# Turning the softmax factors later, reordering the first products, and moving a few loads in a hybrid decoder block

## The chip, the core and the metric

The kernel runs on one core of a Trainium2 chip. A core has a matrix engine, TensorE (in the profile PE, with its weight loads apart as PEld), the vector engine VectorE (DVE), the scalar engine ScalarE (ACT), GpSimd (POOL) and SyncE (SP), whose queue issues most of the DMAs here; ScalarE's queue issues a few. The metric is the device time of one execution in microseconds.

## The reference, cut to what matters

The layer is a macaron block on 1024 tokens of width 1024, all in float32: half a SwiGLU feed-forward, a mixer, and half a second feed-forward, each behind an RMS norm, then a last norm.

```python
h = h + 0.5 * swiglu(rms_norm(h, ffn1_norm), w1, w3, w2)
u = rms_norm(h, mix_norm);  proj = u @ w_in          # q, k, v, p, gates
y_attn = dilated_mixture_attention(q, k, v) @ w_branch_attn
y_pool = multiscale_pool(pz, pool_w, pool_scale) @ w_branch_pool
merged = gates[0] * y_attn + gates[1] * y_pool
h = h + merged @ w_out
h = h + 0.5 * swiglu(rms_norm(h, ffn2_norm), ...)

# dilated_mixture_attention: three groups (window, dilation) of four heads
alpha = softmax(stack(log_denominators), axis=0)      # weights of the groups, per token and head
o = sum(alpha[..., None] * stack(group_outputs), axis=0)
```

The weights `alpha` of the groups are what the kernel calls factors.

## The kernel before, in words

**Products.** Every float32 operand is split into a high part and a low part (`hi`, `lo`), and a product is made of three: high by high, high by low, low by high (`three`, terms 0, 1 and 2, where the first factor is the weight). The large products use a scheme with seven half-size products; tiles are 128 x 512 into one PSUM bank. PSUM has eight banks in two rings of four, with the tags `mm` and `acc`.

**Order.** Inside `tc.manual_schedule()` each engine's instructions stand in the order in which the code emits them; outside of it a planner places them. Each engine, and SP's queue, works its own list in that order.

**The start.** `begin_up1` begins the first feed-forward while x and the first weights still arrive. `run_first(n, ks, terms)` (L1150) issues products of bank n (0 and 1, for two weight matrices) over the chunks ks of the contraction. The first call takes chunks 0 and 1, the second takes chunks 2 and 3 of bank 0 and then of bank 1. In x, `high` (L1057, ScalarE) makes xhi and `low` (L1066, VectorE) makes xlo. `split_low` (L1148, GpSimd) makes the weights' low parts.

**Attention.** 48 slots, one for a pair of heads hp (0, 1), a group g and a block i of 128 queries, are worked in 24 steps q of two slots each: `uses` are the six runs of eight slots. Step q issues in this order: `send()` (stores that are due), on even q the scores of q and q+1 (L1968), pieces of `combines`, a piece of the branch product (`fill`), the transposes of step q-1 (`trans_p`, L2015), more pieces of `fill`, the values of q-2 (L2048), the copy of q-3 out of PSUM (`gather`, L2071), the mask and the maxima (`masked`, L1986, VectorE), the split of the transposed scores of q-1 (ehi L2027 on ScalarE, elo L2030 on VectorE), splits of the next ring of queries and keys (L1590, L1591), `end_branches`, the exponents of both slots (L1995, ScalarE), and last `house` for each slot, which holds the loads and the steps of the factors.

**The factors of the first head pair.** `make_factors(0, gp)` (L1894) is a generator that `house` advances at the slots 32 to 36: the differences to the common maximum; their exponents; the factors (POOL, L1908 to L1912, with a reciprocal on VectorE); the transpose on TensorE (`f_turned`, L1917), its copy on ScalarE (L1919) and its store to DRAM (L1920, `f_by_head`); then four loads that spread the rows over the partitions (L1928, `f_of`). Slot 35 is the last of step q=17. At slot 36 `house` also issues the next values (`load_values`, L1611) and statistics (`get_stats`, L1889), behind the row loads.

**Their use.** `combine(0, half)` runs on GpSimd: per group a multiplication by f_of (L2081) and, from the second group on, an addition (L2085), then ScalarE's copy (L2090) and GpSimd's subtraction (L2091). The steps q = 20 to 23 advance the two halves; the last piece of half 1 stands behind the loop. The second head pair does the same on VectorE with factors that TensorE turns (`factor_rows`, L1946).

**The pooled branch.** `branches()` gives 48 pieces of four matmuls, three to a bank (L2110); behind each bank `end_branches` multiplies by the gate (`gb`, L2124, VectorE), and after each second one `send` stores the result (`by_pool`, L2134).

**Merges.** 16 merges each read a gate and a stored pool result (`load_merge`, L2161 and L2162). Loads 0 and 1 are issued behind the attention loop, load 2 in a closing loop over n = 0 to 7, loads 3 and 4 behind that loop, and from there each merge issues the load five ahead. The output projection (`wo`, L2368) takes its first operand from the first two merges; its split (o_hi L2355, o_lo L2356) is written behind merge 3.

**The second norm's gain** is loaded by `load_gain` (L206) on ScalarE's queue into a tile that held the attention's mask; outside the manual schedule.

Of the kernel before, what the change touches and what calls it, by code (L numbers as in the profile page):

```python
# [19 lines left out]
NT = S // P  # L20
# [117 lines left out]
def tile_block(  # L138
# [67 lines left out]
    def load_gain(src, name):  # L206
        t = keep.tile([P, D], F32, tag="gain", bufs=1, name=f"gain_{name}")
        nc.scalar.dma_start(t, src.to_broadcast([P, D]))
        return t
# [824 lines left out]
    def begin_up1():  # L1034
# [115 lines left out]
        def run_first(n, ks, terms):  # L1150
            if n not in banks:
                banks[n] = quads[n].bank["x"] = bank("mm", f"u_first{n}")
            w, (hi, lo) = first[n], X["b11"]
            for i in terms:
                for k in ks:
                    r = slice(k * P, (k + 1) * P)
                    a, b = three((w[:, 0, r], w[:, 1, r]), (hi[:, k, :], lo[:, k, :]))[i]
                    pe.matmul(banks[n], a, b, start=(k == 0 and i == 0), stop=(k == 3 and i == terms[-1]))

        FRONT, BACK = slice(0, 2 * P), slice(2 * P, HALF)  # L1160
        high("b11", 0, xt(0, 0), gain(0))
# [31 lines left out]
            high("b11", k, xt(0, k), gain(k))  # L1193
        for k in (2, 3):
            low("b11", k, xt(0, k), gain(k))
        run_first(0, (2, 3), (0, 2, 1))
        run_first(1, (2, 3), (0, 2, 1))
        operand(2, 1)
        operand(3, 1)
        high_b21(4)  # L1200
# [186 lines left out]
    class Mix:  # L1387
# [56 lines left out]
        def send(self):  # L1444
            for a in range(2):
                nc.sync.dma_start(gate_dram[self.g][:, a], self.y[a])
# [447 lines left out]
    def make_factors(hp, eng):  # L1894
# [19 lines left out]
        if hp == 0:  # L1914
            yield
            p = bank("mm", "f_turned")[:GROUPS * 2 * NT, :P]
            pe.transpose(p, by_head.rearrange("p g a i -> p (g a i)"), ident)  # L1917
            turned = att_small.tile([GROUPS * 2 * NT, P], F32, name="f_turned")
            ac.activation(turned, p, AF.Copy)  # L1919
            nc.sync.dma_start(f_dram.rearrange("g a i p -> (g a i) p"), turned)  # L1920
            yield
# [264 lines left out]
    def advance(gen, n=1):  # L2186
        for _ in range(n):
            next(gen, None)

    def house(s):  # L2190

        u, i = divmod(s, NT)
        if i == 1 and u > 0 and slots[s - 2][1] != 0:
            send_stats(*slots[s - 2][:2])
        if s - N // 2 in (8, 9, 10, 11, 12):
            advance(factors[0])
        if i == 4 and u + 1 < len(uses):
            load_values(uses[u + 1])
        if u > 0 and i == 4 and slots[s - 5][1] != 0:
            get_stats(*slots[s - 5][:2])  # L2200
        if N - 32 <= s < N - 13:
            advance(first)
        if s in (N - 6, N - 5, N - 4):
            load_ya(s - N + 6)

    first = first_w_o()
    with tc.manual_schedule():
# [6 lines left out]
                    for hp, (adds, lower) in enumerate((((gp, gp), gp), ((gp, ve), ve)))]  # L2214
        splits = {}
        for q in range(N // 2):
            send()
            if q % 2 == 0:
                scores(q)
                scores(q + 1)  # L2220
            for half in {20: (0, 0), 21: (0,), 22: (0, 1), 23: (1, 1)}.get(q, ()):
                advance(combines[0][half])
            if q == 0 or q % 2 == 1:
                next(fill, None)
            if q > 0:
                trans_p(q - 1)
                splits[q - 1] = split_p(q - 1)
                next(fill, None)
                if q % 4 == 1:
                    next(fill, None)  # L2230
            if q > 1:
                values(q - 2)
            if q > 2:
                gather(q - 3)
            masked(2 * q)
            masked(2 * q + 1)
            u, i = divmod(q, NT // 2)
            if 0 < u < len(uses) - 1 and i == 0:
                load_ring(uses[u + 1], ring_place(u + 1))
            if q > 0:  # L2240
                advance(splits[q - 1], 2)
            if i > 1 and 0 < u < len(uses) - 1:
                split_ring(uses[u + 1], i - 2)
                split_ring(uses[u + 1], i)
            end_branches()
            exponents(2 * q)
            exponents(2 * q + 1)
            if q in (2, 3):
                split_ring(uses[1], q - 2)
                split_ring(uses[1], q)  # L2250
            house(2 * q)
            house(2 * q + 1)
# [24 lines left out]
        for n in range(8):  # L2277
            advance(combines[1][n // 4])
            if n not in (3, 5, 7):
                next(fill, None)  # L2280
            end_branches()
            send()
            if n == 3:
                load_merge(2)
        for k in (3, 4):
            load_merge(k)
    assert next(fill, None) is None
    left_b.close()
    xstack.close()
# [3 lines left out]
    late["wc"] = ctx.enter_context(sbuf("wc2"))  # L2293
    late["xa"] = x2.enter_context(sbuf("x2a"))
    late["merged"] = m1.enter_context(sbuf("merged"))
    gain2 = load_gain(ffn2_norm, "ffn2")
    op = wo.enter_context(sbuf("ops", "right"))
    X2 = {}
    fs = ExitStack()
# [89 lines left out]
        return [Rows(X2, "b11", h[t][:, LOWS], t), Rows(X2, "b21", h[t][:, HIGHS], t)]  # L2389

    def scaled2(t):
        scaled(t, h[t] if t < 4 else rows_y[t], gain2)

    def lower(t, rs):
        for r in rs:
# [4 lines left out]
    with tc.manual_schedule():  # L2400
# [20 lines left out]
        for k in range(11, 16):  # L2421
            merge(k)
            if k in (12, 14):
                split_whole(2 + (k - 12) // 2, ve)
        sum_o(4)
        for t in range(4, NT):
            reload(t)
# [260 lines left out]
```

## Time and profile before

| what | value |
|---|---|
| median of 3 runs | 1876.27 us (1876.26 to 1876.63) |
| the profiled execution | 1877.42 us |
| its span, first to last instruction | 1875.2 us |
| TensorE clock granted | 0.999 |
| PE, PEld busy | 1863.7 us (99%), 1545.1 us (82%) |
| DVE, ACT, POOL busy | 1366.2 us (73%), 768.4 us (41%), 783.9 us (42%) |
| DMA | 339.70 MB, mean 181 GB/s |

A row of the timeline has the start and the duration in microseconds, the engine, the line of the kernel, the operation, the tile written and the tiles read, shapes and count, and in brackets how long the engine sat idle before and what released it. A row of the waits has the waiting instruction, the releaser, the total in microseconds, the number of waits and the longest. A row of the windows has a stretch of time and its length, the busy time and count of PE, PEld, DVE, ACT and POOL, then the granted clock, the DMA engines' share and GB/s. The ends of matmuls are modelled, so gaps are better seen in the weight loads.

### The profile page before, as it was taken

The page shows a single profiled execution, that of the slowest core. Times are in us where ns is not written, and L with a number is a line of the kernel's source. Part 1 is how long each engine was busy: PE and PEld are TensorE (multiplying, and loading weights), DVE is VectorE, ACT ScalarE, POOL GpSimd, SP SyncE. Part 2 cuts the span into 40 slices and gives each one's busy share as a digit, 9 for nine tenths or more (in the row PEclk, how much of TensorE's full clock was granted, in tenths as well). Part 3 has the DMA queues.
Part 4 walks back from the last instruction along what each step waited for, and adds up shares of the span by engine and source line. Part 5 has one row for each costly group of instructions (what it writes and reads, how often), then busy time and mean ns, then how long its engine had stood idle before and what let it go on. Part 6 is the DMA issues. An engine that isn't in the chain of part 4 may idle for free.

```text
span 1875.2 us, 24419 instructions
## 1 busy us (share of the span) xinstructions
PE 1863.7 (99%) x8667; PEld 1545.1 (82%) x8667; DVE 1366.2 (73%) x1966; ACT 768.4 (41%) x1393; POOL 783.9 (42%) x569
## 2 busy tenths in 40 slices
PE   9999999999999999999999999999999999999998
PEld 8888888888888888888888887888888888888886
DVE  7887866668886776658885886887765566577867
ACT  7422323233345643334445772463333333343344
POOL 5554644452222364445554467544333333312221
PEclk9999999999999999999999999999999999999999
DMA  8134324356565436765578888634332233354654
GB/s 327 45 124 149 121 95 152 117 206 209 192 231 198 157 114 208 258 211 185 213 251 324 314 254 298 267 129 180 120 139 85 90 107 122 126 203 157 223 197 146
DMA packets 148369, 339.70 MB, mean 181 GB/s; under 512 B 18024, under 2 KB 39576, under 8 KB 146712
## 3 DMA queue, kind: packets, MB, share of 16 engines
q1 hardware_dynamic: 144504, 327.30, 50.1%
q10 hardware_dynamic: 3744, 10.85, 1.6%
q8 instruction: 68, 1.11, 0.2%
q14 instruction: 53, 0.43, 0.1%
HBM read 237.48 MB, written 100.62 MB: 180 GB/s over the span
## 4 chain that ended last, share of the span: by engine, by line
PE 55%; DVE 2%; ACT 2%; DMA 1%; issue 1%; POOL 1%; SPq 0%; ACTq 0%; POOLq 0%; DVEq 0%
PE u_mixm L334 15%; PE d_f L904 8%; PE wo L2368 4%; PE yp L2110 2%; PE o L2048 1%; PE u_f20a L334 1%; PE u_f20b L334 1%; PE u_f21b L334 1%; PE u_f21a L334 1%; PE u_f210b L334 1%; PE u_f210a L334 1%; PE u_f29b L334 1%; PE u_f29a L334 1%; PE u_f28b L334 1%; PE u_f28a L334 1%; PE u_f27b L334 1%
## 5 line engine op out<-in xcount | busy, mean ns | idle before, releaser
L904 PE MATMUL d_f<-bhi_f,ahi_f 128*128 128x512 f32 x616 | 240.2, 390 | 0.0
L904 PE MATMUL d_f<-bhi_f,alo_f 128*128 128x512 f32 x616 | 239.8, 389 | 0.0
L904 PE MATMUL d_f<-blo_f,ahi_f 128*128 128x512 f32 x616 | 239.7, 389 | 0.0
L861 POOL TENSOR_TENSOR alo_f<-g_f,ahi_f 128x512 fp32r<-128x512 f32 x60 | 86.7, 1462 | 269.0 <-ACT ahi_f L857 269.0
L334 PE MATMUL u_mixm<-xhi_t_mix,wc_mixm 128*128 128x512 f32 x608 | 157.3, 391 | 0.1
L904 PEld LDWEIGHTS d_f<-bhi_f,alo_f 128*128 128x128 f32 x616 | 115.6, 188 | 24.3 <-DVE alo_f L861 0.2
L904 PEld LDWEIGHTS d_f<-bhi_f,ahi_f 128*128 128x128 f32 x616 | 115.6, 188 | 24.1 <-ACT h L424 0.5
L904 PEld LDWEIGHTS d_f<-blo_f,ahi_f 128*128 128x128 f32 x616 | 115.7, 188 | 24.0
L334 PEld LDWEIGHTS u_mixm<-xhi_t_mix,wc_mixm 128*128 128x128 f32 x608 | 113.5, 188 | 23.8 <-ACT wc_mixm L322 0.5
L334 PE MATMUL u_mixm<-xhi_b_mix,wc_mixm 128*128 128x512 f32 x456 | 120.3, 391 | 0.0
L325 POOL TENSOR_TENSOR wc_mixm<-s_mixm,wc_mixm 128x512 fp32r<-128x512 f32 x52 | 77.1, 1483 | 101.8 <-ACT wc_mixm L322 95.7
L334 PEld LDWEIGHTS u_mixm<-xhi_b_mix,wc_mixm 128*128 128x128 f32 x456 | 84.9, 188 | 17.2
L322 ACT ACTIVATE wc_mixm<-s_mixm 128x512 fp32r<-128x512 f32 x76 | 47.0, 628 | 111.4 <-DVE s_mixm L378 56.4
L857 ACT ACTIVATE ahi_f<-g_f 128x1024 fp32r<-128x1024 f32 x84 | 81.9, 975 | 6.8 <-DMA g_f<-gs_f 6.6
L334 PE MATMUL u_mixm<-xlo_t_mix,wc_mixm 128*128 128x512 f32 x304 | 81.3, 389 | 0.0
L325 POOL TENSOR_TENSOR wc_mixm<-raw,wc_mixm 128x512 fp32r<-128x512 f32 x41 | 62.3, 1522 | 37.9 <-ACT wc_mixm L322 24.6
L2368 PE MATMUL wo<-w_o,o_hi 128*128 128x512 f32 x224 | 69.4, 391 | 0.0
L646 POOL TENSOR_TENSOR y_f<-y_f,norm_ffn 128x512 f32<-128x512 f32 x35 | 54.4, 1560 | 35.5 <-DVE y_f L627 25.2
L857 ACT ACTIVATE bhi_f<-s_f2w 128x512 fp32r<-128x512 f32 x55 | 32.9, 627 | 86.0 <-DVE s_f2w L879 69.6
L857 ACT ACTIVATE bhi_f<-s_f1w 128x512 fp32r<-128x512 f32 x55 | 33.1, 629 | 83.5 <-DVE s_f1w L879 70.8
L334 PEld LDWEIGHTS u_mixm<-xlo_t_mix,wc_mixm 128*128 128x128 f32 x304 | 57.1, 188 | 12.0
L861 DVE TENSOR_TENSOR alo_f<-g_f,ahi_f 128x1024 fp32r<-128x1024 f32 (+1 forms) x48 | 58.6, 1222 | 7.7 <-ACT ahi_f L857 7.7
(1360 smaller groups left out, 4823.4 us busy)
## 6 DMA issues: line engine op xcount, KB each, us to landing
g_f<-gs_f SPq DMA_DIRECT2D x70, 512.0 KB
gs_f<-y_f SPq DMA_DIRECT2D x88, 256.0 KB
raw<-in_w2a_dram SPq DMA_DIRECT2D x35, 512.0 KB
raw<-in_w2b_dram SPq DMA_DIRECT2D x35, 512.0 KB
gs_f<-gb_f SPq DMA_DIRECT2D x46, 256.0 KB
raw<-in_w1b_dram SPq DMA_DIRECT2D x22, 512.0 KB
raw<-in_w3b_dram SPq DMA_DIRECT2D x22, 512.0 KB
raw<-in_w1a_dram SPq DMA_DIRECT2D x20, 512.0 KB
```

The costliest lines, as they stand in the source:

```text
L322: ac.activation(w[:, 0], src, AF.Copy)
L325: eng.tensor_tensor(w[:, 1], src, w[:, 0].bitcast(F32), op=OP.subtract)
L334: pe.matmul(p, a, b, start=(start and n == 0), stop=(n == 11), skip_group_check=not start)
L646: gp.tensor_tensor(c, c, self.sv.norm[:, cols], op=OP.mult)
L857: ac.activation(hi[:, c], src, AF.Copy)
L861: eng.tensor_tensor(lo[:, d], src[:, o], hi[:, d].bitcast(F32), op=OP.subtract)
L904: pe.matmul(self.banks[m][t], l, r, start=(first and q == 0), stop=(last and q == 2))
L2048: pe.matmul(p, l, r, start=(j == 0), stop=(j == end))
L2110: pe.matmul(p, a, b, start=(j == 0), stop=(j == 11))
L2368: pe.matmul(banks[m][t], l, r, start=(st == 0 and j == 0 and q == 0), stop=(st == 1 and j == 1 and q == 2))
```

## The change

- `run_first` for chunks 2 and 3: the terms 0 and 2 (those with xhi) of both banks first, then term 1 (with xlo) of both.
- The factors of the first head pair: the transpose moves from the end of step q=17 (slot 35) to the middle of step q=18, behind `trans_p`; a new `yield` parts it from the copy and the store, which move to slot 36, behind that step's exponents. The four row loads, and behind them the values and the statistics that slot 36 loaded, move to the head of q=19.
- The pieces of `combine` in q=22 and q=23 change places: two products of half 1 come first, then the last piece of half 0 with one of half 1.
- Merge loads 3 and 4 are issued in the closing loop, at n = 4 and n = 5.
- The gain of the second norm is loaded behind the last merge, inside the manual schedule.

```diff
@@ run_first
-                    pe.matmul(banks[n], a, b, start=(k == 0 and i == 0), stop=(k == 3 and i == terms[-1]))
+                    pe.matmul(banks[n], a, b, start=(k == 0 and i == 0), stop=(k == 3 and i == 1))
...
-        run_first(0, (2, 3), (0, 2, 1))
-        run_first(1, (2, 3), (0, 2, 1))
+        for terms in ((0, 2), (1,)):
+            for n in (0, 1):
+                run_first(n, (2, 3), terms)
@@ make_factors
             pe.transpose(p, by_head.rearrange("p g a i -> p (g a i)"), ident)
+            yield
             turned = att_small.tile([GROUPS * 2 * NT, P], F32, name="f_turned")
@@ house
-        if s - N // 2 in (8, 9, 10, 11, 12):
+        if s - N // 2 in (8, 9, 10, 12):
             advance(factors[0])
-        if i == 4 and u + 1 < len(uses):
+        if i == 4 and u + 1 < len(uses) and s != N // 2 + 12:
             load_values(uses[u + 1])
-        if u > 0 and i == 4 and slots[s - 5][1] != 0:
+        if u > 0 and i == 4 and slots[s - 5][1] != 0 and s != N // 2 + 12:
             get_stats(*slots[s - 5][:2])
@@ the attention loop
         for q in range(N // 2):
+            if 2 * q == N // 2 + 14:
+                advance(factors[0])
+                load_values(uses[(N // 2 + 12) // NT + 1])
+                get_stats(*slots[N // 2 + 7][:2])
             send()
...
-            for half in {20: (0, 0), 21: (0,), 22: (0, 1), 23: (1, 1)}.get(q, ()):
+            for half in {20: (0, 0), 21: (0,), 22: (1, 1), 23: (0, 1)}.get(q, ()):
                 advance(combines[0][half])
...
                 splits[q - 1] = split_p(q - 1)
+                if 2 * q == N // 2 + 12:
+                    advance(factors[0])
                 next(fill, None)
@@ the closing loop
             send()
-            if n == 3:
-                load_merge(2)
-        for k in (3, 4):
-            load_merge(k)
+            if n in (3, 4, 5):
+                load_merge(n - 1)
@@ the gain
-    gain2 = load_gain(ffn2_norm, "ffn2")
...
-        scaled(t, h[t] if t < 4 else rows_y[t], gain2)
+        scaled(t, h[t] if t < 4 else rows_y[t], late["gain"])
...
                 split_whole(2 + (k - 12) // 2, ve)
+        late["gain"] = load_gain(ffn2_norm, "ffn2")
         sum_o(4)
```

## The prediction

> **What bounds the kernel now.** I read the page first: the shares of the engines beside the span.
>
> ```profile
> span 1875.2 us, 24419 instructions
> ## 1 busy us (share of the span) xinstructions
> PE 1863.7 (99%) x8667; PEld 1545.1 (82%) x8667; DVE 1366.2 (73%) x1966; ACT 768.4 (41%) x1393; POOL 783.9 (42%) x569
> ```
>
> TensorE is busy for all but 11.5 us (1875.2 - 1863.7). An edit that takes no matmul away can win only gaps in that stream, so I went next to the view of waits, for the weight loads, where gaps show a little larger than in the modelled matmuls.
>
> ```profile
> PEld wo L2368 <- DVE o_lo L2356: 1.6, 2, 1.2
> PEld u_first L1158 <- DVE xlo_b_f L1066: 1.4, 1, 1.4
> PEld o L2048 <- DVE elo L2030: 1.3, 2, 0.8
> PEld idle L1041 <- DVE fours L1042: 1.1, 1, 1.1
> PEld f_turned L1917 <- POOL f L1912: 0.8, 1, 0.8
> ```
>
> Columns: total us, times, longest. Three of these lie where the diff works: u_first (the first products of the first feed-forward), f_turned (the turned softmax factors), and wo (the output projection, whose first operands come out of the merges). Together they are 1.4 + 0.8 + 1.6 = 3.8 us, and 0.2% of 1876.27 is 3.75 us, which is about what a measurement of this kernel can tell from no change. So even the whole of them would barely show.
>
> **Part 1, the first products.** The stall in the timeline of matmuls (start, duration), and GpSimd's last split of the weights:
>
> ```profile
> 11.75 0.50 PE L1158 MATMUL u_first<-xlo_b_f,wc_first 128*128 128x512 f32 x1 [0.98 <-DVE xlo_b_f L1066]
> 12.09 1.10 PE L1158 MATMUL u_first<-xhi_b_f,wc_first 128*128 128x512 f32 x4
> 13.03 0.62 PE L1158 MATMUL u_first<-xlo_b_f,wc_first 128*128 128x512 f32 x2
> 13.49 0.40 PE L334 MATMUL u_f11a<-xhi_b_f,wc_f11a 128*128 128x512 f32 x1
> ```
>
> ```profile
> 7.93 1.44 POOL L1148 TENSOR_TENSOR wc_first<-raw,wc_first 128x256 fp32r<-128x256 f32 x2
> ```
>
> Nothing is added or removed; 12 matmuls are reordered. Before, bank 0 runs its four products with xhi, then its two with xlo, and the second of these waits until 11.75; only then come the six of bank 1. After, the four xhi products of bank 1 stand ahead of all xlo products. Their weights were ready at 7.93 + 1.44 = 9.37, so they fill the gap. Four matmuls cost 13.03 - 12.09 = 0.94 us and the gap in matmuls is 0.98, so **-0.94**; the last xlo is still awaited at 11.75. Bounds: -0.98 if the gap closes wholly, and 0 if the lead is lost again, for which there is a place:
>
> ```profile
> 58.21 0.53 PEld L334 LDWEIGHTS u_f10a<-xhi_t_f,wc_f10a 128*128 128x128 f32 x3 [0.51 <-ACT wc_f10a L322]
> ```
>
> Here TensorE waits for ScalarE. If ScalarE's work there is paced by TensorE, it comes 0.94 earlier too; if not, the wait grows from 0.51 to 1.45. I take -0.94, since the waits view names no DMA as releaser of TensorE anywhere.
>
> **Part 2, the factors.** Before, the turn, its ScalarE copy and its store stand at the end of an odd step (q=17); TensorE waits for GpSimd there. After, the transpose stands behind the next step's own transposes, the copy behind that step's exponents, and the four row loads at the head of q=19. What moves: one matmul, one ACTIVATE and eight transfers on SP's queue (the store, four row loads, and behind them two value loads and one of statistics). The SP rows, then the ScalarE rows at which the new copy will stand, and the VectorE row that gives a score bank back:
>
> ```profile
> 1096.83 0.33 SPq L1920 DMA_DIRECT2D f_by_head<-f_turned  x1
> 1097.27 0.36 SPq L2134 DMA_DIRECT2D by_pool<-gb  x1
> 1098.31 2.61 SPq L1928 DMA_DIRECT2D f_of<-f_by_head  x4
> ```
>
> ```profile
> 1101.65 0.19 ACT L1995 ACTIVATION_READ_ACCUMULATOR e<-e,own_stats 128x1 f32 x1
> 1102.26 0.60 ACT L2027 ACTIVATE ehi<-tp 128x512 fp32r<-128x512 f32 x1 [0.42 <-PE tp L2015]
> ```
>
> ```profile
> 1097.98 0.08 DVE L1986 DVE_READ_ACCUMULATOR2_ANT own_stats<- 128x1 f32 x1
> ```
>
> The stall of 0.8 goes, so the step runs 0.8 earlier. The exponents end at 1101.84 - 0.8 = 1101.04. The copy is taken at 0.3 and hides in ScalarE's idle 0.42. The transpose now comes behind the four banks of scores and needs the first of them back, which VectorE has read at 1098.06 today; at most 0.8 (the whole win) is lost on that, and I take nothing, since TensorE's next transposes wait for the exponents anyway. The store goes out at about 1101.3, and the first row load follows as before by 1098.31 - 1096.83 = 1.48, at 1102.8: 4.5 us later than now. The by_pool store, queued behind the factors' store today, passes it.
>
> Who waits for the rows? GpSimd's eleven operations that combine the first head pair:
>
> ```profile
> 1096.00:1098.00 2.00, 1.80 (x26) 1.60 (x27) 1.51 (x9) 0.27 (x1) 0.15 (x1) 1.00 0.05 12
> 1098.00:1102.00 4.00, 3.89 (x23) 2.95 (x23) 2.96 (x9) 3.17 (x11) 2.14 (x2) 1.00 0.67 228
> 1102.00:1106.00 4.00, 4.00 (x40) 3.55 (x41) 3.49 (x16) 3.17 (x11) 2.93 (x4) 1.00 1.07 240
> ```
>
> ```profile
> 1103.46 2.53 POOL L1591 TENSOR_TENSOR xhi_b_mix<-xhi_b_mix,xlo_b_mix 128x512 fp32r<-128x512 f32 x2 [1.07 <-ACT xlo_b_mix L1590]
> 1105.94 2.56 POOL L2081 TENSOR_TENSOR o<-o,f_of 128x512 f32<-128x512 f32 x2
> ...
> 1113.24 1.27 POOL L2091 TENSOR_TENSOR att<-o,att 128x512 fp32r<-128x512 f32 x1 [0.74 <-ACT att L2090]
> ...
> 1119.73 1.29 POOL L2085 TENSOR_TENSOR o<-o,o 128x512 f32<-128x512 f32 x1
> ```
>
> The last columns of the windows are the DMA share and GB/s. Today GpSimd starts at 1105.94, straight behind its earlier work, and ends the chain at 1119.73 + 1.29 = 1121.02, 15.08 later with a wait of 0.74 inside. The first half needs two of the four row loads: by the code 64 x 3 x 512 x 4 bytes each, 0.79 MB for two. At the mean of 228 and 240 GB/s that is 3.4 us, and the store issued at 1097.27 moved hardly a byte before 1098.0, which I read as 0.7 of start-up. So the rows land at about 1102.8 + 0.7 + 3.4 = 1106.9. The reordered pieces (half 0 is finished behind the first products of half 1) take the 0.74 out, so the chain ends at 1106.9 + 15.08 - 0.74 = 1121.2, against 1121.02. Does the end of this chain matter?
>
> ```profile
> 1121.06 0.63 ACT L2090 ACTIVATE att<-o 128x512 fp32r<-128x512 f32 x1
> 1121.56 0.34 ACTq L208 DMA_DIRECT2D gain_ffn<-in_ffn_norm_dram  x1
> 1121.60 0.58 ACT L2027 ACTIVATE ehi<-tp 128x512 fp32r<-128x512 f32 x1
> ```
>
> ```profile
> 1124.69 2.00 ACT L1937 ACTIVATE f_of<-f 128x1024 f32<-128x1024 f32 x2 [1.89 <-DVE f L1912]
> ...
> 1125.93 0.35 PEld L1946 LDWEIGHTS fa<-ident,f_of 128*128 128x128 f32 x3
> ```
>
> It does: ScalarE copies its result (L2090, within 0.04 of GpSimd's end), then splits the last scores (ehi), behind which VectorE makes the second pair's factors, ScalarE spreads them, and TensorE turns them at 1125.93. The first of the two copies at 1124.69 ends about 1125.7, so 0.2 is free. A chain 0.2 later less 0.2 free leaves fa where it was, and the 0.8 won at q=18 is waited out here: **0.0**. Bounds: -0.8 if nothing in this chain binds; +3.3 by the first rival below. The activation that finishes half 0 (0.63, as L2090 at 1121.06) moves from q=22 to q=23 with its GpSimd subtraction; it stands ahead of the same kind of work, and its price is in the sum of the eleven operations.
>
> The row was 1.48 from a store to the reads of what it wrote. The Trainium skill ("DMA: Bandwidth & Descriptors", section "Anatomy of one DMA") gives a fixed cost of some 2.0 us for a DMA, most of it until the written data is confirmed; by that the rows would come 0.5 later and this part would cost 0.5 instead of nothing. I go by the row.
>
> The two value loads behind the rows (1.05 MB) are used here:
>
> ```profile
> 1115.24 0.28 PE L2048 MATMUL o<-ehi,v_in 128*128 128x256 f32 x1
> ```
>
> Rows and values are 2.6 MB, through by 1102.8 + 0.7 + 11.2 = 1114.7 at the same rate, against 1115.24 - 0.8 = 1114.4; the 0.3 comes out of the same 0.8.
>
> **Part 3, the merge loads.** Loads 3 and 4 are written into the loop over n, at n = 4 and 5, rather than behind it. Is there a store between? These rows tell:
>
> ```profile
> 1133.30 0.68 DVE L2083 TENSOR_TENSOR o<-o,fa 128x512 f32<-128x512 f32 x1
> 1133.89 0.68 DVE L2124 TENSOR_TENSOR gb<-yp,gb 128x512 f32<-128x512 f32 x1
> 1134.50 0.68 DVE L2083 TENSOR_TENSOR o<-o,fa 128x512 f32<-128x512 f32 x1
> ```
>
> ```profile
> 1134.60 0.32 SPq L2134 DMA_DIRECT2D by_pool<-gb  x1
> ```
>
> The last branch's product (gb) stands between the multiplications of n = 4 and n = 5, so its store is issued by the send of n = 4: 48 branch pieces, 42 taken in the main loop, two behind it, four at n = 0, 1, 2, 4. In the new code the load of n = 4 still comes behind that send. The queue of SP keeps its order, store then loads, and the 1.6 us at wo stay: **0.0**, at best -1.6.
>
> **Part 4, the gain.** Its load leaves ScalarE's queue at 1121.56 (0.34, overlapping two activations that run back to back there) and goes behind the last merges. It moves 128 x 1024 x 4 bytes, 0.52 MB, 2.2 us of DMA time at the 234 GB/s above, in either place. It is not used before the norm that follows the output projection, so only its company can suffer: **0.0**, at most 0.3 either way (about its 0.34 on ScalarE).
>
> **Sum.** -0.94 + 0.0 + 0.0 + 0.0 = -0.94 on the profiled execution: 1877.42 (span 1875.2 and 2.2 around it) becomes 1876.5. That execution lies 1.15 above the median 1876.27; the same step from the median gives **1875.3**.
>
> **Rivals.** *The rows come late, and the kernel gets slower.* If GpSimd's first multiplication needs all four row loads, or the stream runs at half its rate, they land at 1102.8 + 0.7 + 6.7 = 1110.2 and the chain ends at 1110.2 + 14.34 = 1124.5, which is 3.5 later than now, less 0.2 free = +3.3; with -0.94 that is +2.4, or 1878.7. It decides from a start of 1107.8 on, where the chain's delay passes 0.94 + 0.2. For it: SP's store comes 4.4 late into a DMA stream that is full (share 1.07). Against it: today GpSimd starts at 1105.94, when 0.91 + 0.96 = 1.87 MB had moved since 1098.0, less than the store and four row loads (2.1 MB), so it cannot have waited for all four. The Trainium skill's advice (same page, "Rules for kernel authors") to issue a DMA early and wait for it late speaks for this rival, too: the reads move towards their user.
>
> *The start's gain is lost at 58.21*, where ScalarE may not follow: total 0.0, 1876.3. *The 0.8 is kept*, when the end of the attention isn't bound by GpSimd's chain: -1.74, 1874.5. For it, nothing waits visibly at 1125.93; against it, the 0.04 between GpSimd and ScalarE. *The merge loads do pass the store*, against my count: -0.94 - 1.6 gives 1873.7.
>
> **Chances.** Forecast 0.55; late rows 0.15; start lost 0.12; 0.8 kept 0.13; merge loads 0.05. The range reaches from 1874.3, just under the case that keeps 0.8, to 1877.4, half way into the late rows; the forecast's own is 1874.9 to 1875.8. None of the cases crosses 0.2%: faster than 1872.5 needs two best cases at once (0.02), slower than 1880.0 late rows and late values together (0.04), so 0.94 for no change.
>
> **What would show it.** Right: u_first gone from the waits or under 0.3, u_f11a starting near 12.55; no wait at f_turned; the store of f_by_head near 1101 less the start's lead; GpSimd's first multiplication of L2081 near 1106; SP's order store, merge, merge unchanged and wo waiting as before. Wrong: a GpSimd wait of over 2 us for a DMA before L2081, a wait of TensorE at fa or at values of q=22 above 1 us, or merge loads ahead of the store.

## The result, and the profile after

The changed kernel takes 1879.28 us (median of 20 runs, 1878.00 to 1880.68) and the kernel before 1876.26 us on the same chip (20 runs, 1875.23 to 1877.89): a ratio of 1.0015, with a 95% interval from 1.0009 to 1.0021. It is 3.0 us slower where 0.94 less was forecast (under the 0.2% that the prediction took as the least that can be told, yet the interval leaves out 1), and it lies beyond the range's upper end, near the rival in which the rows come late (1878.7). The profiled execution after took 1878.00 (span 1875.8), the quickest of its kernel; the one before took 1877.42, near the slow end of its range. The two spans differ by 0.6 only, so the profiles were taken a second time below. Line numbers after are one higher from L1199 on, two higher from L1920 to L2216, and five or more higher behind that.

The waits of the profile after, in the stretch from 1090 to 1150 us (total, times, longest):

```profile
POOL o L2083 <- DMA f_of<-f_by_head: 4.5, 1, 4.5
ACT att L2092 <- POOL o L2087: 2.2, 1, 2.2
DVE top L1904 <- DMA stats<-st: 1.6, 1, 1.6
PEld fa L1948 <- ACT f_of L1939: 1.5, 1, 1.5
PEld o L2050 <- DMA v_in<-v: 1.4, 1, 1.4
PEld wo L2373 <- DVE o_lo L2361: 0.6, 1, 0.6
PEld f_turned L1918 <- issue: 0.3, 1, 0.3
```

The stall at f_turned has shrunk from 0.8 to 0.3. In its place stand three waits for transfers: GpSimd for the rows of factors, TensorE for the values of q=22, VectorE for the statistics of the last group (the second head pair's factors need them). GpSimd's wait and TensorE's two are the prediction's own signs of "wrong". The queues of SP and GpSimd in that trace, and its windows (last columns: granted clock, DMA share, GB/s):

```profile
1099.84 0.33 SPq L1922 DMA_DIRECT2D f_by_head<-f_turned  x1
1101.32 2.59 SPq L1930 DMA_DIRECT2D f_of<-f_by_head  x4
...
1117.76 0.38 SPq L1890 DMA_DIRECT2D stats<-st  x1
```

```profile
1108.34 2.55 POOL L2083 TENSOR_TENSOR o<-o,f_of 128x512 f32<-128x512 f32 x2 [4.54 <-DMA f_of<-f_by_head]
...
1121.29 1.29 POOL L2087 TENSOR_TENSOR o<-o,o 128x512 f32<-128x512 f32 x1
```

```profile
1096.00:1102.00 6.00, 5.87 (x41) 4.74 (x39) 5.17 (x20) 5.27 (x18) 3.27 (x3) 1.00 0.03 8
1102.00:1104.00 2.00, 2.00 (x28) 1.83 (x26) 1.96 (x9) 1.36 (x8) 1.80 (x2) 1.00 0.34 106
1104.00:1106.00 2.00, 2.00 (x13) 1.75 (x12) 1.77 (x5) 2.00 (x8) 0.00 (x0) 1.00 0.88 226
1106.00:1108.00 2.00, 2.00 (x13) 1.73 (x12) 1.96 (x7) 1.52 (x5) 0.00 (x0) 1.00 1.06 221
```

The transfer engines stand idle for six microseconds (share 0.03) because the store waits for ScalarE's copy, which now comes behind the exponents. Then the rows take 7.0 us from the first load's issue (1101.32) to GpSimd's start (1108.34). GpSimd's chain ends at 1122.58, and the profile shows what hangs on it, ScalarE first, then TensorE:

```profile
1122.62 0.63 ACT L2092 ACTIVATE att<-o 128x512 fp32r<-128x512 f32 x1 [2.21 <-POOL o L2087]
1123.15 1.07 ACT L2029 ACTIVATE ehi<-tp 128x512 fp32r<-128x512 f32 x2
1124.11 0.24 ACT L1907 ACTIVATE w<-w 128x48 f32<-128x48 f32 x1
```

```profile
1127.34 0.66 PE L1948 MATMUL fa<-ident,f_of 128*128 128x128 f32 x4 [1.26 <-ACT f_of L1939]
```

### The profile page after: what moved, and what is told of

The parts are those of the page before. It is cut to its first block, busy times and chain, and to the rows that moved or that the text cites. A ratio compares the mean times of both kernels' runs of the same rounds, so it can differ in the third digit from the quotient of the medians.

```text
span 1875.8 us, 24418 instructions
## 1 busy us (share of the span) xinstructions
PE 1863.3 (99%) x8667; PEld 1544.1 (82%) x8667; DVE 1364.0 (73%) x1966; ACT 768.3 (41%) x1393; POOL 784.2 (42%) x569
## 4 chain that ended last, share of the span: by engine, by line
PE 53%; DVE 2%; DMA 2%; ACT 2%; issue 1%; POOL 1%; SPq 0%; ACTq 0%; DVEq 0%; POOLq 0%
PE u_mixm L334 15%; PE d_f L904 8%; PE wo L2373 4%; PE u_f20a L334 1%; PE u_f21b L334 1%; PE u_f20b L334 1%; PE u_f21a L334 1%; PE u_f210b L334 1%; PE u_f210a L334 1%; PE u_f29b L334 1%; PE u_f29a L334 1%; PE u_f28b L334 1%; PE u_f28a L334 1%; PE u_f27b L334 1%; PE u_f27a L334 1%; PE u_f26b L334 1%
```

## The experiments

All times are medians; a ratio is to the kernel before, timed beside it on the same chip, with its 95% interval. Each profile is of one execution. There are four theories. **G** (first called R): the rows are late, GpSimd's chain behind them ends late, and that sets the end of the attention. **Q**: the transfers form one line from the first row to the last group's statistics, so those come late as well, and VectorE's wait sets the end. **V**: TensorE's wait for the values does; **C**: the loss is in the closing part.

### Each part alone

`e_start` is Part 1 alone, `e_factors` Part 2 alone, `e_late` Parts 3 and 4 alone, `e_no_factors` Parts 1, 3 and 4; their diffs are those pieces of the change.

> Part 1 alone, everything else as before. Theory R (the rows of factors land late and GpSimd's chain behind them sets the end of the attention) and theory V (the values of q=22 land late and TensorE's wait for them sets it) both say that the loss of the changed kernel is all in Part 2, and the start keeps what the trace after shows from u_f11a on: 1.2 us ahead of before, through the whole kernel, 1875.1 us. Theory C (the loss is in the closing part: the merge loads and the gain) says the same. If the lead is lost where before already waited for transfers (merge loads, 2.1 us on VectorE at the end of the attention), the time is that of before, 1876.3.

> Part 2 alone, without the 1.2 us that Part 1 gives. Theory R: the first row load is issued near 1102.5, two row loads land 6.9 us behind it, GpSimd starts near 1109.4 and ends its chain 14.2 us later near 1123.7, fa is 2.7 us behind before: 1878.1 where the closing part gives 0.9 back as in the trace after, up to 1880.5 where it gives nothing back and the median of after is carried over. Theory V: the stall of 1.0 at f_turned goes, a wait of 1.65 for the values comes: 1876.9. Theory C: nothing, 1876.3 or 1.0 less.

> Parts 3 and 4 alone. Theories R and V: no change, 1876.3 +- 0.5, with the order store, merge, merge on SP as before. Theory C: the loss of the changed kernel is here, 1878.5 or more, with a longer wait for a merge load or for the gain.

> Parts 1, 3 and 4 together, Part 2 left as before. Theories G and Q: the whole loss goes; the sum of what Part 1 alone (0.3 under before) and Parts 3 and 4 alone (0.7 under before) gave is 1.0 under before, 1875.2; 1876.0 if the 0.7 was chance. Any loss left against before would mean that the parts hinder each other.

| kernel | median | before | ratio |
|---|---|---|---|
| e_start | 1875.90 | 1876.22 | 0.9999 (0.9990 to 1.0008) |
| e_factors | 1880.27 | 1876.22 | 1.0022 (1.0014 to 1.0031) |
| e_late | 1875.55 | 1876.22 | 0.9997 (0.9988 to 1.0006) |
| e_no_factors | 1875.54 | 1876.74 | 0.9996 (0.9987 to 1.0005) |

Part 2 alone costs 4.05; the other parts give 0.3 and 0.7, which no interval tells from nothing. The sum, 4.05 - 0.3 - 0.7 = 3.05, is the loss of the changed kernel. C falls. The 1.2 us expected of Part 1 didn't come either, and the start of `e_factors`, which doesn't hold Part 1, says why: there u_f11a begins at 12.55, though it began at 13.49 before.

### The same two kernels profiled again

> The kernel before, profiled a second time, because its start in the runs of Part 2 alone and of Parts 3 and 4 alone has no gap of 0.98 us at u_first though Part 1 isn't in them. If that gap belongs to the one execution profiled first: u_f11a starts near 12.5 instead of 13.49, VectorE's wait for a merge load at the end of the attention is near 1.0 instead of 2.1, span near 1874. If it belongs to the kernel: 13.5 and 2.1 again, span 1875.

> The changed kernel, profiled a second time. Theory G (GpSimd's chain behind the late rows alone sets the end of the attention): GpSimd idle 4 to 5 us for the rows, fa 1.4 behind the first profile of before, as in the first profile of after. Theory Q (one transfer queue runs without a gap from the first row to the statistics of the last group, so each microsecond by which the first row starts later reaches those statistics, and VectorE's wait for them sets the end as often as GpSimd does): VectorE waits 1.6 to 3.3 us for the statistics at its factors, and fa comes between 1.4 and 2.7 behind.

One execution each: before 1876.73 (span 1874.5), after 1880.84 (span 1878.6). The opening in the timeline of matmuls, second profile of before:

```profile
10.82 0.50 PE L1158 MATMUL u_first<-xlo_b_f,wc_first 128*128 128x512 f32 x1
11.16 1.10 PE L1158 MATMUL u_first<-xhi_b_f,wc_first 128*128 128x512 f32 x4
12.11 0.62 PE L1158 MATMUL u_first<-xlo_b_f,wc_first 128*128 128x512 f32 x2
12.56 1.09 PE L334 MATMUL u_f11a<-xhi_b_f,wc_f11a 128*128 128x512 f32 x4
```

and the profile after:

```profile
11.39 1.08 PE L1158 MATMUL u_first<-xlo_b_f,wc_first 128*128 128x512 f32 x4
12.31 1.07 PE L334 MATMUL u_f11a<-xhi_b_f,wc_f11a 128*128 128x512 f32 x4
```

The gap of 0.98 isn't there the second time. It belonged to one execution. Over all profiles u_f11a starts at 12.25 on average with Part 1 (15 of them, 12.02 to 12.55) and at 12.50 without (four, the first left out): Part 1 is worth about 0.25 at this place; that it reaches the end isn't shown. VectorE's wait for a merge load at the end of the attention was 1.8 in the second profile of before, not near 1.0 as expected, and 0.6 to 2.6 over all of them: it, too, changes from run to run.

The same matmul's start, second profile of before taken as zero (negative is ahead):

| where | after | after, again |
|---|---|---|
| step 17, ahead of the factors | -0.23 | -0.07 |
| step 20, the stall at f_turned gone | -1.23 | -1.06 |
| behind the values of q=22 | +0.41 | +0.77 |
| fa | +2.29 | +3.39 |
| first output projection, behind the merges | +1.82 | +3.88 |

So the lead won at f_turned is 1.0, and about 3.5 and 4.5 are lost from there to fa. VectorE and GpSimd in the second profile of after show what the first hid:

```profile
1120.37 1.16 DVE L1903 TENSOR_TENSOR top<-stats 128x16 f32<-128x16 f32 x1
1123.55 0.18 DVE L1904 TENSOR_TENSOR top<-top,stats 128x16 f32<-128x16 f32 x1 [2.02 <-DMA stats<-st]
1123.76 1.19 DVE L1905 TENSOR_TENSOR w<-top,stats 128x48 f32<-128x48 f32 x1
```

```profile
1121.57 1.28 POOL L2087 TENSOR_TENSOR o<-o,o 128x512 f32<-128x512 f32 x1
1123.60 1.29 POOL L2093 TENSOR_TENSOR att<-o,att 128x512 fp32r<-128x512 f32 x1 [0.74 <-ACT att L2092]
```

```profile
1124.99 0.24 ACT L1907 ACTIVATE w<-w 128x48 f32<-128x48 f32 x1 [0.49 <-DVE w L1905]
```

The same steps of VectorE and ScalarE in the second profile of before, where neither waits (lines one lower):

```profile
1120.12 0.18 DVE L1903 TENSOR_TENSOR top<-top,stats 128x16 f32<-128x16 f32 x1
```

```profile
1121.58 0.24 ACT L1906 ACTIVATE w<-w 128x48 f32<-128x48 f32 x1
```

In the second profile of after GpSimd ends its chain at 1122.85, but the exponential of the second factors comes only at 1124.99, straight behind VectorE's L1905 (1123.76 + 1.19 = 1124.95). In the first profile it came at 1124.11, behind ScalarE's own split. Two chains end within a microsecond of each other, and either can be last.

### The copy moved, early or late

`v_early`: the changed kernel with the copy and store behind ehi, and rows, values and statistics in slot 36 again.

```diff
-        if i == 4 and u + 1 < len(uses) and s != N // 2 + 12:
+        if i == 4 and u + 1 < len(uses):
...
-        if u > 0 and i == 4 and slots[s - 5][1] != 0 and s != N // 2 + 12:
+        if u > 0 and i == 4 and slots[s - 5][1] != 0:
...
-            if 2 * q == N // 2 + 14:
-                advance(factors[0])
-                load_values(uses[(N // 2 + 12) // NT + 1])
-                get_stats(*slots[N // 2 + 7][:2])
...
                 advance(splits[q - 1], 2)
+            if 2 * q == N // 2 + 12:
+                advance(factors[0])
```

> The changed kernel with the copy and the store of the factors directly behind step 18's first ScalarE copy (behind ehi, ahead of the operand splits and the exponents), and rows, values and statistics back in slot 36. Theory R: copy near 1097.0 instead of 1099.55, first row load near 1098.8 instead of 1101.3, rows land near 1105.7, GpSimd ends near 1120.0, so fa comes 1.0 us ahead of before instead of 1.4 behind: 1875.3, or 1.0 below before's median of the same chip. Theory V: values land 2.5 us sooner too, TensorE keeps its lead of 2.2: 1874.1 if nothing else binds. Theory C: no change from after, 1879.3.

1878.42, ratio 1.0009 (1.0000 to 1.0018): about a quarter of the loss goes, not all of it. TensorE's wait for the values is gone, and fa came at 1127.01, hardly sooner than after (1127.34): V falls. SP waited longer for the factors' store (the first row load was issued 2.40 behind it instead of 1.48), so that load went out at 1099.83; and VectorE waited 3.3 us for the statistics.

`b_copy_late`: the kernel before, with only the copy moved behind the exponents of step 18, and rows, values and statistics to the head of step 19.

```diff
             pe.transpose(p, by_head.rearrange("p g a i -> p (g a i)"), ident)
+            yield
...
+            if 2 * q == N // 2 + 14:
+                advance(factors[0])
+                load_values(uses[(N // 2 + 12) // NT + 1])
+                get_stats(*slots[N // 2 + 7][:2])
```

> The kernel before with one step of Part 2 alone: the copy and the store of the factors come behind step 18's exponents, and rows, values and statistics at the head of step 19, while the transposition with its stall of 0.8, the order of the combines and everything else stay. Theories G and Q: this alone brings the whole loss, because TensorE's lead wasn't on the path: the first row load near 1102.5 and fa 2.5 to 3.5 behind before: 1879.5 (1879 to 1880.5). If the mere lateness of the transfers costs less than 1.5, the rest of Part 2 (the order of the combines, the transposition's new place) has a share of its own.

1881.59, ratio 1.0026 (1.0015 to 1.0037): the late copy alone brings the whole loss and 2 us more than the changed kernel. The size was missed: without the lead of the other edits the copy came at 1101.78, and a second wait appeared, ScalarE's for GpSimd's first half in step 22:

```profile
1117.24 0.63 ACT L2091 ACTIVATE att<-o 128x512 fp32r<-128x512 f32 x1 [5.35 <-POOL o L2086]
```

`v_old_order`: the changed kernel with the combines as before.

```diff
-            for half in {20: (0, 0), 21: (0,), 22: (1, 1), 23: (0, 1)}.get(q, ()):
+            for half in {20: (0, 0), 21: (0,), 22: (0, 1), 23: (1, 1)}.get(q, ()):
```

> The changed kernel with the combines in the order of before (first half's copy and subtraction in step 22, second half's last two multiplications in step 23). GpSimd stood idle 0.74 us for ScalarE's copy there in the trace of before, and doesn't in the trace after. Theory G: GpSimd ends 0.7 later, fa 2.1 behind the first profile of before instead of 1.4: 1880.0. Theory Q: where VectorE's wait for the statistics decides, nothing changes: between 1879.3 and 1880.0. If ScalarE waits in step 22 for GpSimd's first half and the exponents behind it come late, TensorE loses up to 2 us of its lead, which isn't on the path either.

1879.53, ratio 1.0015 (1.0006 to 1.0024): the time of the changed kernel. ScalarE waits 5.4 us for GpSimd in step 22, and GpSimd's chain is 15.0 long instead of 14.2; fa came at 1128.20, between the two profiles of after. The new order avoids a stall that late rows make (in the profile before, the same wait was 0.65).

`v_mid`: the transposition between the scores and the first transposition of step 18, copy and store at once; rows, values and statistics in slot 36, as in `v_early`.

```diff
                 scores(q + 1)
+            if 2 * q == N // 2 + 12:
+                advance(factors[0], 2)
...
                 splits[q - 1] = split_p(q - 1)
-                if 2 * q == N // 2 + 12:
-                    advance(factors[0])
```

> The changed kernel with the transposition of the factors in step 18 between the scores and the first transposition of the exponents, the copy and the store directly behind it (ahead of step 18's first ScalarE copy), and rows, values and statistics in slot 36. TensorE still doesn't stall for the factors. First row load near 1098.1 and first row moving near 1099.6, as early as before (1099.8). Theory Q: VectorE's wait for the statistics falls from 3.3 (copy behind ehi) and 1.6 (changed kernel) to under 0.5, GpSimd starts near 1105.1 and ends near 1119.5, fa comes 1.0 to 1.6 ahead of the first profile of before: 1875.0 (1874.5 to 1875.6). Theory G: the same start and end of GpSimd, and the same time. If the time stays above 1877, neither holds.

1876.99, ratio 1.0002 (0.9993 to 1.0010). Above the forecast: the transposition stalled 0.8 in its new place as well, the first row load went out at 1099.15, GpSimd started at 1106.30, VectorE still waited 0.6 for the statistics, and then L1905 took 1.24.

### A queue of their own for the statistics

`after_q` is the changed kernel and `v_mid_q` is `v_mid`, with store and load of the last merged group's statistics issued by ScalarE.

```diff
+        queue = nc.scalar if (hp, g) == slots[N - 9][:2] else nc.sync
-            nc.sync.dma_start(d, v)
+            queue.dma_start(d, v)
```

> The changed kernel with the statistics of the last merged group (store and load) issued by ScalarE, so that they stand in a transfer queue of their own and not behind rows, values and late weights in SP's. Rows and values stay as late as in the changed kernel (GpSimd starts near 1108.4). Theory G: nothing changes, 1879.3, fa 1.4 to 2.5 behind the first profile of before. Theory Q: VectorE no longer waits for statistics (1.6 and 2.0 us in the two profiles of after), its factors are ready before GpSimd ends, and fa comes 1.4 behind in every run: 1878.4, 0.5 to 1.0 under the changed kernel; the rest of the loss stays, being GpSimd's.

> The version with the factors transposed between the scores and the first transposition, copied and stored at once, with the statistics of the last merged group by ScalarE's queue as well. Without the second edit VectorE waited 0.6 us for the statistics and then 1.2 us each for two small operations that ended together with GpSimd's. Theory Q with that contention: the statistics are there before step 23, VectorE's factors are done early, ScalarE's exponential follows its split copy without the wait of 0.5: fa 0.5 sooner than without the edit, near the first profile of before, 1876.3. Theory G: GpSimd's end decides alone, no change, 1876.9.

1879.28, ratio 1.0012 (1.0003 to 1.0021), and 1877.17, ratio 1.0005 (0.9996 to 1.0014): no change, and no answer, since the edit didn't free the statistics. VectorE still waited 2.8 and 2.0 us for them. (In the profiled execution of `after_q`, 1880.39, the store and the rows also came 1.9 later than in the first profile of after.) The transfers of `after_q` from 1118 to 1124 us:

```profile
DMA packets 2559, 2.05 MB, mean 342 GB/s; under 512 B 1140, under 2 KB 2374, under 8 KB 2558
q1 hardware_dynamic: 1519, 2.02, 98.5%
q10 hardware_dynamic: 1039, 0.02, 11.9%
```

The 16 KB of statistics are 1024 small packets in ScalarE's queue (q10), spread over these six microseconds beside 2 MB of late weights in SP's (q1). The expectation overlooked a rule of the Trainium skill ("DMA: Bandwidth & Descriptors", section "Issuing engines are not separate DMA queues"): transfers of different issuers share the same 16 engines. This trace agrees.

### Two by two: the statistics freed, GpSimd's chain shortened

`after_ya` issues six loads of late weights three slots later, behind the statistics; `after_short` leaves out two of GpSimd's multiplications (2.6 us); `after_short_ya` has both; `v_early_ya` is `v_early` with the first.

```diff
-        if s in (N - 6, N - 5, N - 4):
-            load_ya(s - N + 6)
+        if s in (N - 3, N - 2, N - 1):
+            load_ya(s - N + 3)
...
             if hp == 0:
-                gp.tensor_tensor(o[g], o[g], f_of[hp][:, g, c], op=OP.mult)
+                if half == 0 or g == 2:
+                    gp.tensor_tensor(o[g], o[g], f_of[hp][:, g, c], op=OP.mult)
```

> The changed kernel with the six loads of late weights (1.5 MB) that stand in SP's queue around the last group's statistics issued three slots later, behind them. Theory G (GpSimd's end plus 1.5 us of ScalarE gives the exponential of the second factors, and the rest follows): VectorE's wait for the statistics goes, fa comes 1.5 + 3.45 us behind GpSimd's end as in the first profile of after: at most 0.5 under the changed kernel, 1878.8 to 1879.3. Theory Q (the statistics in the queue decide): 1 us or more under it, 1878.2.

> The changed kernel without two of GpSimd's six multiplications by the factors (first and second group, second half of the tokens, first pair of heads), so its chain is 2.6 us shorter; statistics and late weights as in the changed kernel. Theory G: GpSimd ends near 1120.0 and fa comes 2.6 sooner: 1876.7. Theory Q: VectorE still waits for the statistics until 1122.9 to 1123.6, the exponential comes near 1123.3 to 1124.0, fa comes 0.8 to 1.0 sooner: 1878.4.

> Both edits: two of GpSimd's multiplications left out and the late weights issued behind the statistics. Theories G and Q: with both chains shorter fa comes 2.6 sooner, 1876.7. If it stays above 1878, a third thing sets the end of the attention in the changed kernel (the values that TensorE waits for).

> The version with the copy directly behind ehi, where VectorE waited 3.3 us for the statistics, and GpSimd ended at 1121.4, with the late weights behind the statistics. Theory Q: the wait goes, and fa comes 2.0 sooner, 1876.4. Theory G: the exponential can't come before GpSimd's end plus 1.5 us, 1122.95 instead of 1123.57: 0.6 sooner, 1877.8.

From the timelines (GpSimd's end is the last addition's start and duration; statistics: VectorE's second minimum; w: the end of VectorE's L1905):

| kernel | GpSimd starts | ends | statistics | w | exponential | fa | median, ratio |
|---|---|---|---|---|---|---|---|
| before, again | 1104.97 | 1120.06 | 1120.12 | 1120.54 | 1121.58 | 1125.05 | 1876.26 |
| after | 1108.34 | 1122.58 | 1122.87 | 1123.29 | 1124.11 | 1127.34 | 1879.28, 1.0015 |
| after, again | 1108.61 | 1122.85 | 1123.55 | 1124.95 | 1124.99 | 1128.44 | |
| after_ya | 1108.90 | 1123.14 | 1121.81 | 1123.21 | 1124.67 | 1127.90 | 1878.52, 1.0011 |
| after_short | 1108.35 | 1119.98 | 1123.60 | 1124.02 | 1124.05 | 1127.50 | 1878.13, 1.0012 |
| after_short_ya | 1108.54 | 1120.16 | 1120.54 | 1120.95 | 1121.93 | 1125.61 | 1875.90, 1.0000 |
| v_early | 1107.07 | 1121.41 | 1122.14 | 1123.54 | 1123.57 | 1127.01 | 1878.42, 1.0009 |
| v_early_ya | 1106.64 | 1120.95 | 1119.62 | 1121.02 | 1122.48 | 1125.71 | 1876.73, 1.0005 |

Intervals of the four new ratios: 1.0002 to 1.0020, 1.0003 to 1.0021, 0.9991 to 1.0009, 0.9996 to 1.0014. One row each of VectorE and ScalarE in `after_short`, where GpSimd is done early and the statistics are not:

```profile
1123.60 0.18 DVE L1904 TENSOR_TENSOR top<-top,stats 128x16 f32<-128x16 f32 x1 [3.47 <-DMA stats<-st]
```

```profile
1124.05 0.24 ACT L1907 ACTIVATE w<-w 128x48 f32<-128x48 f32 x1 [2.20 <-DVE w L1905]
```

and the same in `after_short_ya`:

```profile
1120.54 0.17 DVE L1904 TENSOR_TENSOR top<-top,stats 128x16 f32<-128x16 f32 x1 [0.21 <-DMA stats<-st]
```

```profile
1121.93 0.24 ACT L1907 ACTIVATE w<-w 128x48 f32<-128x48 f32 x1
```

Freeing the statistics alone takes 0.8 off the changed kernel's median, shortening GpSimd alone 1.2, both together 3.4. Neither of the first two is clear of the changed kernel by the intervals; both together give the time of the kernel before. By the expectations `after_ya` fell between Q's 1878.2 and G's 1878.8, `after_short` came near Q's 1878.4, and `after_short_ya` 0.8 under its 1876.7. In seven of the eight rows the exponential is the later of two: GpSimd's end + 1.5, or w + 0.03. In `after_short_ya` ScalarE reaches it at its own pace. The rule also holds, within 0.03, in the twelve profiles that the table leaves out. TensorE's wait for the values of q=22 was still 1.4 in `after_short_ya`, so V falls here too. So neither G nor Q alone: the late rows delay two chains by about as much, each hides behind the other, and a cure of one is worth little. `v_early_ya` came between the two forecasts (1876.4 and 1877.8), nearer to Q's: its statistics landed in time, GpSimd's end + 1.5 (1122.48) then decided, as G says, and GpSimd itself ended 0.5 sooner than in `v_early`. With the late weights out of the way the early copy costs nothing against before that the interval can tell (1.0005), which fits.

### The stall filled with other work

`e_fill` is `e_no_factors` with the branch products of step 18 ahead of the transposition in slot 35; `e_fill_swap` has the new order of the combines too.

```diff
+        if s == N // 2 + 11:
+            next(fill, None)
         if s - N // 2 in (8, 9, 10, 11, 12):
             advance(factors[0])
...
                 splits[q - 1] = split_p(q - 1)
-                next(fill, None)
+                if 2 * q != N // 2 + 12:
+                    next(fill, None)
```

> Parts 1, 3 and 4, with the transposition of the factors, copy, store and rows where before has them, and the four pooled-branch products of step 18 moved ahead of the transposition, where TensorE stood 0.8 us. TensorE gains 0.7 there, and the rows come at most 0.3 later than before. By the account of the runs so far (the exponential of the second factors comes 1.5 us behind GpSimd's end or directly behind the statistics, and TensorE waits for what follows), GpSimd's end doesn't move, so TensorE's 0.7 is waited out at fa: 1875.5, as Parts 1, 3 and 4 alone. If TensorE's lead alone were worth something: 1874.8.

> The same with the combines in the order of the changed kernel (GpSimd's chain 14.2 instead of 15.1 us). GpSimd ends 0.6 to 0.8 sooner than before, TensorE comes 0.7 sooner too, so fa comes 0.5 to 0.7 sooner: 1874.9 (1874.6 to 1875.4). If the statistics, landing where they land before, hold VectorE instead: 1875.5.

1876.60, ratio 1.0000 (0.9991 to 1.0008), and 1876.66, ratio 1.0002 (0.9993 to 1.0011): nothing won. TensorE had its stall filled, but SP waited for the factors' store in `e_fill`

```profile
SPq L1929 <- DMA f_by_head<-f_turned: 2.2, 1, 2.2
```

where it had waited 0.6 in `e_no_factors`, so the rows began 1.6 later than in the second profile of before (1098.92 instead of 1097.32, in both). GpSimd started 0.7 and 0.9 later, and in `e_fill_swap` its chain (14.8 instead of 15.1) didn't make up for that. The question that `e_fill_swap` was to settle, whether TensorE's lead and a shorter chain of GpSimd together win anything, stays open. No version in this document is faster than the kernel before by its interval; the best ratio is that of `e_no_factors`, 0.9996 (1875.54 beside 1876.74).

## Why the prediction was wrong

**Part 1** (-0.94). The direction held, the size didn't: about 0.25. u_f11a starts at 12.31, earlier than the 12.55 forecast, but a kernel without the edit starts it at 12.50. The step that failed is the reading of 0.98 as the kernel's. The prediction noted that the profiled execution lay 1.15 above the median and still took a gap of that execution off the median. The wait that the prediction showed at 58.21 is 0.51 in both profiles after as before, so no lead is lost there, and that rival falls.

**Part 2** (0.0, bounds -0.8 to +3.3). Its links were right and one term was mis-sized. Right: the first row load 1.48 behind the store, the store's place behind the exponents, GpSimd's end deciding ScalarE's copy, the chain of 14.3 (measured 14.24). The Trainium skill's 2.0 us ("DMA: Bandwidth & Descriptors", section "Anatomy of one DMA", which measures it for DMAs that GpSimd issues, while SP issues these) would have put the rows 0.5 later. In the trace after the 1.48 of the row came back; four other kernels had 2.4 to 3.1.

The step that failed is the landing of the first two row loads: 0.7 of start-up and 3.4 for 0.79 MB at the mean rate, 4.1 in all. Each of these transfers reports in 16 parts, and the traces keep the times of the reports; it has landed with the last one. In the first profile of after the four row loads landed at 1106.30, 1108.20, 1110.01 and 1111.76, and GpSimd started 0.14 behind the second. So two loads were needed, as the prediction said, but the second landed 6.9 behind the first one's issue (1101.32). The kernel before was no faster: there the second landed at 1105.50, 7.2 behind the first one's issue (1098.31). GpSimd showed no wait because it started at 1105.94, straight behind other work; the room was 0.44, and the rows' issue moved by 3.0. With 7.2 in place of 4.1 the prediction's own sum comes, as an estimate, to a chain that ends at 1102.8 + 7.2 + 14.34 = 1124.3, 3.3 later than in before, and to 1878.5.

Where the 2.8 between 4.1 and 6.9 lie: the loads behind the first landed 1.75 to 1.90 apart, near the 1.7 of the mean rate. The first landed 4.98 behind its issue, where 0.7 + 1.7 = 2.4 was counted. Its first packet ran 1.42 behind its issue, in before as well; the 0.7 had been read from the start of a store. And its 16 parts ended far apart, from 1104.83 to 1106.30: by the windows above 2.0 x (0.106 + 0.226) = 0.66 MB had moved by 1106.0, when its 0.39 MB were still not complete, so parts of the later loads had gone ahead of its last ones. By 1108.0 it was 1.1 MB, with 0.79 not complete. Why the parts of a load end so far apart was not tried.

The rival named for this gave the right sign and nearly the right size, 1878.7 against 1879.28, but that is luck in part: GpSimd did start past its turning point of 1107.8, yet neither of its conditions held. GpSimd didn't wait for the third and fourth load, and 0.39 MB every 1.8 us is not half of 234 GB/s. Its +3.3 at fa stands beside +2.5 and +3.5 in the two profiles after, each corrected by its own start.

Left out altogether: the statistics of the last group. The prediction counted the transfers that were moved and not those behind them. SP issues the load of these statistics when their store has landed. In the second profile of before the store landed at 1113.91 and the load at 1118.64, 1.5 ahead of its use; in the first of after at 1117.75 and 1122.77, and VectorE waited. They cost nothing as long as GpSimd is later, and 0.6 in the second profile after (exponential at 1124.99; GpSimd's end + 1.5 is 1124.4). The values of q=22 came late as well: TensorE's weight loads waited 1.4 and 1.3 for them, where 0.3 was forecast; `v_early`, without that wait, was hardly quicker at fa, so TensorE's lead was worth nothing at this place.

**Part 3** (0.0). As forecast. SP's queue after:

```profile
1136.14 0.32 SPq L2136 DMA_DIRECT2D by_pool<-gb  x1
1136.51 1.66 SPq L2163 DMA_DIRECT2D merge<-gate  x1
```

The store still stands ahead. The wait at wo (1.6 before, 0.6 after) isn't a gain of this part: it was 1.7 in the second profile of after and 0.5 in `e_start`, which lacks the part, and Parts 3 and 4 alone are 0.9997. **Part 4** (0.0): as forecast, by the same run; the two were not timed apart.

## What to carry to other kernels

A step that feeds a transfer is priced by the transfer's landing and by everything queued behind it, not by the engine that runs it. An engine that shows no wait for a transfer may have started just behind its landing, so look up the landing in the trace before, and take the difference as the room. Here a copy of 0.3 us moved by 3 us delayed two chains by as much. A stall of one engine is worth removing only if every other chain that meets it downstream has room, and where two chains tie, test them together, since a cure of one shows a fraction of the gain. Before a gap of one profile enters a sum, look for it in a second one.

## What the hardware showed beside that

**Small VectorE operations beside GpSimd's.** L1903 and L1905 (128x16 and 128x48) take 0.16 to 0.21 us when GpSimd idles and up to 1.3 when they start beside one of its operations, by how much of it is left; they end with it (second profile of after: 1120.37 + 1.16 = 1121.53, and GpSimd's next starts at 1121.57; 1124.95 beside 1123.60 + 1.29 = 1124.89). The profile shows it as a long duration, not as a wait. The Trainium skill ("SBUF — State Buffer", section "SBUF: two separate sides") says that an operation of VectorE with two inputs in SBUF and one of GpSimd that reads SBUF exclude each other through a shared port, and the loser waits for the whole instruction. The rows agree. In the first profile of after L1905 fell into GpSimd's pause of 0.74 and took 0.21, in the second it didn't and took 1.19.

**A small store can take 1 to 1.5 us longer to land.** The first row load, which waits for the 24 KB of f_by_head, was issued 1.5 to 1.6 us behind that store in most kernels, 2.4 in `v_early` and `v_early_ya`, and 3.1 in `e_fill` and `e_fill_swap`. Loads of instructions (8 and 16 KB) ran among those transfers at the time; that they held the store's last packets was not tried.
